# Attention visited once a turn, and three output tiles in front of the last operand, in a two-block fp32 transformer kernel on one core

## The chip, the cores and the metric

The kernel runs on one core of a Trainium2 chip, as one launch. Its time is the device time in microseconds (us); beside it stands the span of a profiled execution, from its first to its last instruction. Engines go by their short names: PE is the matrix engine (TensorE), DVE the vector engine, ACT the scalar engine, POOL GpSimd, SP the engine whose queue issues most DMAs.

## The reference

One sequence of 512 tokens with 1024 features goes through two blocks, all in float32. The first block has one layer:

```python
h = rms_norm(x, norm_mix); z = h @ w_in          # q, k, v of two attentions and two gates
y_a = windowed_gqa(q_a, k_a, v_a, sink)          # 8 heads, window of 128 on both sides
y_b = neighborhood_attn(q_b, k_b, v_b, rpb)      # 8 heads, 8 x 16 neighbourhood on an 8 x 64 grid
x = x + (gate_a * (y_a @ w_proj_a) + gate_b * (y_b @ w_proj_b)) @ w_out
x = x + square(relu(rms_norm(x) @ w_up)) @ w_down    # 4096 hidden features
```

and a norm at its end. The second block has two layers, each of which is

```python
x = x + 0.5 * swiglu(rms_norm(x), wg, wu, wd)    # 2816 hidden features
z = rms_norm(x) @ w_in                           # q, k, v, and three inputs of a convolution
attn = sliding_window_attention(q, k, v, sink)   # 8 query heads, 2 key heads, blocks of 128, causal
conv = b_gate * causal_conv3(c_gate * h_conv)
x = x + concatenate([attn, conv]) @ w_out
x = x + 0.5 * swiglu(rms_norm(x), wg, wu, wd)
```

and then a last norm.

## The kernel before

Activations lie with features on the 128 partitions and the 512 tokens along the free axis, in 8 blocks of features. To keep float32 accuracy every operand is split in two halves, a rounded high part and the rest as a low part (`wh`, `wl` for weights), and each product of blocks is three matmuls, high by high, high by low, low by high (L463 to L465 for a linear layer). A linear tile is 128 outputs by 512 tokens and sums over 8 operands, so it has 24 matmuls; it lies in one of three accumulator banks of PSUM (`acc`), or for the last tiles of an output linear in another.

Weights come in one stream in the order in which they are used. A tile has two items, each for four operands. An item is split by a cast on ACT (L389, the high half) and a subtraction on DVE (L391, the low half) into a pair of buffers of a ring of 7 (`RING`). The order of instructions on every engine is that in which the program issues them; nothing is reordered later. Splits are issued only in `split_to`: when a tile fetches an item, `item` asks for splits up to 5 items ahead (`AHEAD`), and `split_to` cuts this to 6 items behind the oldest item that is still in use. When the last item of a 512 KB unit is split, SP gets the DMA of a later unit, into one of 5 raw buffers.

`linear2` runs tiles side by side: all operands but the last `late` of each tile first, then the late operands of each tile, and then the evacuations. `out_linear` uses it for the first two tiles of an output linear (`ORDER` = 0, 1, 4, 2, 5, 3, 6, 7), with the last operand late; it runs the other six tiles one by one with `linear`, which issues a tile's matmuls, then what is due (the squares for the next norm), then its evacuation. There are three output linears: `wo` of the first block, with the operands in the order 0 to 7, and `0_wo` and `1_wo` of the second block's layers, with the operands in the order 4, 5, 6, 7 (convolution) and 0, 1, 2, 3 (attention). An evacuation (`ev_res`, L962) adds the tile to the residual `x` and then prepares the next feed-forward's operands (`prep_pairs`): for outputs 0 to 3 by four instructions on ACT (L656 to L661) and three on DVE, for outputs 4 to 7 by three on ACT (L666 to L672) and five longer ones on DVE (L667 to L674).

`run_attention` goes through the 16 steps of an attention in turns. A step is scores (`qk`, L782, which contract over 64 partitions, two heads at once), softmax (`soft` on ACT and its second half on DVE), transposes of the probabilities (`tr`, L823) and values (`pv_`, L843). In the second block (`late` true) a step's transposes come two turns behind its scores and its values three, so there are 19 turns. Between them PE works on the fill: the tiles of the other projections, cut in pieces of two operands (6 matmuls). Which pieces run where is set by shares of the total. A tile that ends goes on the list `evacs`, and `evacuate` issues its evacuation. A turn before the change is: scores; `evacuate`; fill up to half the turn's share; values; transposes; softmax; splits; the softmax's second half; fill up to the turn's share. The first block's two attentions run by the same function with `late` false.

Of the kernel before, what the change touches and what calls it, by code (L numbers as in the profile page):

```python
# [32 lines left out]
MID = 0.5  # L33
SLACK = (0.3, 0.2)
# [7 lines left out]
ORDER = [0, 1, 4, 2, 5, 3, 6, 7]  # L42
# [195 lines left out]
def two_blocks(ctx, tc, plan, xT, wstream, vecs, sinks, rpb_g, dists, masks, outT):  # L238
# [59 lines left out]
    def give(ids):  # L298
        for i in ids:
            if i in plain:  # L300
                plain.remove(i)
                use_slot(i, F32R)
        free.extend(ids)
        free.sort()
# [13 lines left out]
    for i in range(4):  # L318
        s = slot[7 * i:7 * i + 7]
# [50 lines left out]
    def split_item(idx):  # L370
        key, part = items[idx]
        combine(idx)
        h = wt_p.tile([P, S], F32R, tag="wh", name=f"wh{idx}")
        lo = wt_p.tile([P, S], F32R, tag="wl", name=f"wl{idx}")
        if blocks[key][0] is not None:
            (u, off), = where[key]
            k0, k1 = parts_of(key, part)
            src = raw[u][:, off + P * k0:off + P * k1]
        else:
            ra, rb = raw[where[key][0][0]], raw[where[key][1][0]]  # L380
            new = sums_of.get(key, {})
            if key[1] == "R":
                src = (ra, rb)[part % 2][:, S * (part // 2):S * (part // 2) + S]
            else:
                src = {1: ra[:, :S], 2: ra[:, S:], 4: rb[:, S:]}.get(part)
                if src is None:
                    src = new[{5: "s1", 6: "s2", 7: "s3", 3: "s4"}[part]]
        w = src.shape[1]
        nc.scalar.copy(h[:, :w], src)  # L389
        combine(idx + 1)  # L390
        nc.vector.tensor_tensor(lo[:, :w], src, h[:, :w].bitcast(F32), ALU.subtract)  # L391
        ready[idx] = (h, lo)
        for u, _ in where[key]:
            uses[u] -= 1
            if uses[u] == 0:
                raw.pop(u)
                freed.append(u)
        while freed and min(freed) == st["oldest"]:
            freed.remove(st["oldest"])
            st["oldest"] += 1  # L400
            load_unit()
# [4 lines left out]
    def split_to(idx):  # L406
        oldest = min(live) if live else st["next"]
        idx = min(idx, oldest + RING - 1, len(items) - 1)
        while st["split"] <= idx:
            split_item(st["split"])  # L410
            st["split"] += 1
# [81 lines left out]
    def flush():  # L493
        todo, deferred[:] = deferred[:], []
        for f in todo:
            f()

    def evacuate():
        todo, evacs[:] = evacs[:], []
        for _, f in todo:  # L500
            f()

    def linear(key, opnd, evac, pool=None, before=None):
        t = Tile(key, opnd, pool)
        t.mm(range(len(opnd)))
        run_due()
        flush()
        if before:
            before()
        evac(t.ps)  # L510
# [18 lines left out]
    def linear2(keys, opnd, evs, order, late, after=None, at=(0, 3)):  # L529


        n_e = len(order) - late
        t0 = Tile(keys[0], opnd)
        t0.mm(order[:n_e])
        t1 = Tile(keys[1], opnd)
        t1.mm(order[:n_e])
        if n_e:
            t0.mm(order[n_e:])
            t1.mm(order[n_e:])
        else:  # L540
            for part in range(2):
                t0.fetch(part)
                t1.fetch(part)
            for kc in order:
                t0.mm([kc])
                t1.mm([kc])
        if after:
            a, b = at
            t2 = Tile(keys[2], opnd)
            if a:  # L550
                t2.mm(order[:a])
            second = after()
            t2.mm(order[a:b])
            second()
            evs[0](t0.ps)
            evs[1](t1.ps)
            t2.mm(order[b:])
            evs[2](t2.ps)
        else:
            evs[0](t0.ps)  # L560
            evs[1](t1.ps)

    def ft(name):
        return ft_p.tile([P, S], F32, tag="ft", name=name)
# [189 lines left out]
    def preload(func):  # L754
        nc.scalar.activation(dummy, epst, func)
# [96 lines left out]
    def run_attention(steps, fillers, needs, head=1, late=False):  # L852

        n = len(steps)
        lag = LAG2 if late else LAG1
        slots = n + lag + 1
        hold = [] if late else [50, 51]
        assert all(i in free for i in hold)
        free[:] = [i for i in free if i not in hold]
        total = sum(f[1] for f in fillers)  # L860
        parts, have, cost = [], set(), [0.0]
        queue = list(fillers)

        def fill():
            if not parts:
                key, c, make = queue.pop(0)
                fs = make()
                parts.extend((key if i == len(fs) - 1 else None, c / len(fs), f) for i, f in enumerate(fs))
            key, c, f = parts.pop(0)
            cost[0] += c  # L870
            f()
            have.add(key)

        def fill_to(share, slack):
            while (queue or parts) and cost[0] < total * share - slack:
                fill()

        for _ in range(2 * head):
            fill()
        total -= cost[0]  # L880
        cost[0] = 0.0

        for s in range(slots):
            if s < n:
                while not set(needs(s)) <= have:
                    fill()
                if any(key[-len(k):] == k for k in needs(s) for key, _ in evacs):
                    evacuate()
                steps[s][0](steps[s][4])
            evacuate()  # L890
            fill_to((s + MID) / slots, SLACK[0])
            if s > lag:
                k = s - lag - 1
                steps[k][3](steps[k][4])
            if lag <= s < n + lag:
                steps[s - lag][2](steps[s - lag][4])
            if s < n:
                rest = steps[s][1](steps[s][4])
                split_to(st["next"] + 2)
                rest()  # L900
            fill_to((s + 1) / slots, SLACK[1])
        assert not queue and not parts
        evacuate()
        flush()
        give(hold)
# [54 lines left out]
    def ev_res(n, scale, prepare):  # L960
        def f(ps):
            nc.vector.scalar_tensor_tensor(x[n], ps, scale, x[n], ALU.mult, ALU.add)  # L962
            if prepare:
                prepare(n)
        return f
# [36 lines left out]
    late = []  # L1002
# [16 lines left out]
    qa, ya, yb, qb, kb, vb = {0: take(2)}, {}, {}, {}, {}, {}  # L1019
    ka, va = take(2), take(2)  # L1020
    linear2(MIX1_HEAD, xop, [ev_split(qa[0], QS), ev_split(ka), ev_v(va)], ar, KC, make_inv, (5, 7))
    ya_done = []

# [77 lines left out]
    def needs_ab(s):  # L1101
        c = s % 16 // 4
        if s < 16:
            return [("qa", c)] if c else []
        return [("qb", c), ("kb", c), ("vb", c)]

    run_attention([(*f_a, s) for s in range(16)] + [(*f_b, s) for s in range(16)],
                  [fill(k) for k in FILL_AB], needs_ab)

# [23 lines left out]
    LAST_POOL = {ORDER[-2]: (y_p, "y"), ORDER[-1]: (sp_p, "sp")}  # L1133

    def out_linear(prefix, op, order, scale, prepare, before):
        linear2([prefix + ("wo", n) for n in ORDER[:2]], op, [ev_res(n, scale, prepare) for n in ORDER[:2]], order, 1)
        for n in ORDER[2:]:
            linear(prefix + ("wo", n), op, ev_res(n, scale, prepare), LAST_POOL.get(n), before if n == ORDER[-1] else None)
        preload(AF.Sqrt)

# [252 lines left out]
    def mix2(l, before):  # L1393
        qs, ys, tmp = {0: take(2)}, {}, {}
        ks, vs = take(2), take(2)
        linear2([(l,) + k for k in MIX2_HEAD], xop, [ev_split(qs[0], QS), ev_split(ks), ev_v(vs)], ar, 1, make_inv)
        cs = [take(2, late=True) for _ in range(4)]
        nc.vector.tensor_tensor(inv2, inv, inv, ALU.mult)
# [23 lines left out]
        def fl(key):  # L1422
            def make():
                if key[0] == "q":
# [6 lines left out]
                             y_plain(ys, lambda c: qs[c] + (ks + vs if c == 3 else [])),  # L1431
                             alibi(f"c{l}", 384, 256), 1 + l, (-1, 0))
        run_attention([(*f_c, s) for s in range(16)], [fl(k) for k in FILL_C],
                      lambda s: [("q", s // 4)] if s >= 4 else [], late=True)
        both = [ys[c] for c in range(4)] + cs
        out_linear((l,), [pair_of(i) for i in both], [4, 5, 6, 7, 0, 1, 2, 3], 1.0,
                   lambda n: prep_pairs(n, vcols(("ffn2_norm_2", l))), before)
        for i in both:
# [75 lines left out]
```

## Time and profile before

| | |
|---|---|
| median of 3 runs | 2453.61 us (2453.45 to 2454.51) |
| profiled execution | 2451.71 us |
| its span | 2449.6 us, 39694 instructions |
| DMA | 239.47 MB, mean 98 GB/s |
| HBM read, written | 234.81 MB, 2.10 MB |

Weight loads (PEld) run beside matmuls (PE). A line of a timeline is one instruction, or several alike in a row merged (x4); its first number is the start, its second how long it took, and an engine's idle time ahead of it stands in square brackets at its end, with what it waited for. Matmuls are pipelined: the next one starts before the one ahead has ended, so it is the distances of starts that count. In windows PEclk is the granted clock as a share of 2.4 GHz.

### The profile page before, as it was taken

The numbers are of one execution on the slowest core, as the hardware profiler recorded it, in microseconds if no ns is written. First come the engines' busy times: TensorE is split into PE (matmuls) and PEld (weight loads), VectorE is DVE, ScalarE is ACT, GpSimd is POOL, SyncE is SP. The second block draws the span as 40 slices with busy tenths as digits, with TensorE's granted clock in tenths as the row PEclk, the third lists the DMA queues.
The fourth block names the chain that finished last, engine by engine and source line by source line (L and its number), as shares of the span: only waits on it lengthen the run. The fifth ranks groups of instructions, "written<-read, shape, count | busy, mean of one in ns | idle before, by whom it ended". The sixth has DMA issues, their size and how long they took to land.

```text
span 2449.6 us, 39694 instructions
## 1 busy us (share of the span) xinstructions
PE 2434.6 (99%) x15192; PEld 2173.5 (89%) x15192; DVE 1957.1 (80%) x3962; ACT 1258.7 (51%) x2736; POOL 11.6 (0%) x26
## 2 busy tenths in 40 slices
PE   9999999999999999999999999999999999999998
PEld 7888889999889999888899999899999888999997
DVE  7778578877689978768798888898787687988885
ACT  5454355544455545444565445665445444654454
POOL 0000000000000000000000000000000000000000
PEclk9999999999999999999999999999999999999999
DMA  4222432233332333322223333333323222233332
GB/s 162 72 91 90 121 109 82 95 102 97 105 103 87 108 101 102 111 92 70 87 83 100 101 102 111 101 99 96 114 88 115 95 69 78 81 103 106 107 94 80
DMA packets 74622, 239.47 MB, mean 98 GB/s; under 512 B 8768, under 2 KB 10816, under 8 KB 74432
## 3 DMA queue, kind: packets, MB, share of 16 engines
q1 hardware_dynamic: 71248, 228.49, 29.2%
q0 software_dynamic: 1600, 6.82, 0.9%
q8 instruction: 119, 1.95, 0.3%
q10 hardware_dynamic: 1584, 1.64, 0.2%
q14 instruction: 71, 0.58, 0.1%
HBM read 234.81 MB, written 2.10 MB: 97 GB/s over the span
## 4 chain that ended last, share of the span: by engine, by line
PE 95%; DVE 3%; ACT 1%; DMA 0%; issue 0%; DVEq 0%; SPq 0%; ACTq 0%
PE X L1166 7%; PE X L1168 7%; PE X L1167 7%; PE YZ L1166 5%; PE YZ L1168 5%; PE YZ L1167 5%; PE mlp_D L463 2%; PE mlp_D L464 2%; PE mlp_D L465 2%; PE 0, 'ffn1'_D L463 2%; PE 0, 'ffn2'_D L463 2%; PE 1, 'ffn1'_D L463 2%; PE 1, 'ffn1'_D L464 2%; PE 0, 'ffn2'_D L464 2%; PE 0, 'ffn1'_D L464 2%; PE 1, 'ffn1'_D L465 2%
## 5 line engine op out<-in xcount | busy, mean ns | idle before, releaser
L391 DVE TENSOR_TENSOR wl<-raw,wh 128x512 fp32r<-128x512 f32 (+2 forms) x890 | 533.7, 610 | 98.9 <-ACT wh L389 91.3
L389 ACT CAST wh<-raw 128x512 fp32r<-128x512 f32 (+2 forms) x890 | 470.9, 556 | 5.2 <-PE 0, 'ffn1'_D L464 1.0
L1166 PE MATMUL X<-r,wh 128*128 128x256 f32 x1568 | 443.2, 283 | 1.2 <-ACT g L1172 0.7
L1168 PE MATMUL X<-r,wl 128*128 128x256 f32 x1568 | 443.7, 283 | 0.0
L1167 PE MATMUL X<-r,wh 128*128 128x256 f32 x1568 | 443.6, 283 | 0.0
L389 ACT CAST wh<-s 128x512 fp32r<-128x512 f32 x392 | 242.7, 620 | 230.0 <-DVE s L368 225.4
L1166 PE MATMUL YZ<-r,wh 128*128 128x256 f32 x1176 | 333.5, 284 | 0.4
L1167 PE MATMUL YZ<-r,wh 128*128 128x256 f32 x1176 | 332.8, 283 | 0.0
L1168 PE MATMUL YZ<-r,wl 128*128 128x256 f32 x1176 | 332.7, 283 | 0.0
L391 DVE TENSOR_TENSOR wl<-s,wh 128x512 fp32r<-128x512 f32 x392 | 269.5, 687 | 67.2 <-ACT wh L389 65.5
L1166 PEld LDWEIGHTS X<-r,wh 128*128 128x128 f32 x1568 | 300.0, 191 | 11.2 <-ACT g L1172 1.1
L1167 PEld LDWEIGHTS X<-r,wh 128*128 128x128 f32 x1568 | 300.0, 191 | 9.1
L1168 PEld LDWEIGHTS X<-r,wl 128*128 128x128 f32 x1568 | 300.0, 191 | 0.0
L1166 PEld LDWEIGHTS YZ<-r,wh 128*128 128x128 f32 x1176 | 225.7, 192 | 1.1 <-ACT u L1178 1.0
L1167 PEld LDWEIGHTS YZ<-r,wh 128*128 128x128 f32 x1176 | 225.7, 192 | 0.0
L1168 PEld LDWEIGHTS YZ<-r,wl 128*128 128x128 f32 x1176 | 225.7, 192 | 0.0
L1180 ACT COPY g<-X 128x256 f32<-128x256 f32 x98 | 36.5, 373 | 137.5 <-PE X L1168 137.4
L1181 DVE TENSOR_TENSOR u<-u,g 128x256 f32<-128x256 f32 x98 | 41.6, 425 | 73.6 <-ACT g L1180 73.1
L463 PE MATMUL mlp_D<-r,wh 128*128 128x512 f32 x256 | 100.1, 391 | 0.0
L464 PE MATMUL mlp_D<-r,wh 128*128 128x512 f32 x256 | 100.1, 391 | 0.0
L465 PE MATMUL mlp_D<-r,wl 128*128 128x512 f32 x256 | 99.6, 389 | 0.0
L1176 ACT COPY u<-X 128x256 f32<-128x256 f32 x98 | 36.5, 373 | 96.6 <-PE X L1168 96.3
(436 smaller groups left out, 5246.7 us busy)
## 6 DMA issues: line engine op xcount, KB each, us to landing
raw<-in_w SPq DMA_DIRECT2D x318, 512.0 KB, 3.6
raw<-in_w SPq DMA_DIRECT2D x64, 384.0 KB, 3.4
raw<-in_w SPq DMA_DIRECT2D x32, 448.0 KB, 3.7
raw<-in_w SPq DMA_DIRECT2D x32, 320.0 KB, 2.9
raw<-in_w SPq DMA_DIRECT2D x32, 256.0 KB, 2.7
bb<-in_rpb POOLq DMA_DIRECT2D x12, 384.0 KB, 3.5
xt<-in_x POOLq DMA_DIRECT2D x8, 256.0 KB, 2.9
xt<-in_x SPq DMA_DIRECT2D x2, 512.0 KB, 6.5
```

Of the source, the lines that this page charges most:

```text
L389: nc.scalar.copy(h[:, :w], src)
L391: nc.vector.tensor_tensor(lo[:, :w], src, h[:, :w].bitcast(F32), ALU.subtract)
L463: nc.tensor.matmul(self.ps, h[:, c], hx, start=(self.n == 1), stop=False)
L464: nc.tensor.matmul(self.ps, h[:, c], lx, start=False, stop=False)
L465: nc.tensor.matmul(self.ps, lo[:, c], hx, start=False, stop=end)
L1166: nc.tensor.matmul(out, h[:, c], hx, start=first, stop=False, skip_group_check=skip)
L1167: nc.tensor.matmul(out, h[:, c], lx, start=False, stop=False, skip_group_check=skip)
L1168: nc.tensor.matmul(out, l[:, c], hx, start=False, stop=(k == 3), skip_group_check=skip)
L1176: nc.scalar.copy(u[:, lo], out)
L1180: nc.scalar.copy(g[:, hi], out)
L1181: nc.vector.tensor_tensor(u[:, hi], u[:, hi], g[:, hi], ALU.add)
```

## The change

Three places change. `linear2` takes a list of tiles instead of two (where it is given an `after`, it takes two as before). `out_linear` gives it three tiles instead of two. And in `run_attention`, for the second block alone, a turn becomes: values; transposes; scores; softmax; `evacuate`; splits; the softmax's second half; fill up to the turn's share. What a turn's scores need is still filled and evacuated ahead of all this.

```diff
         n_e = len(order) - late
-        t0 = Tile(keys[0], opnd)
-        t0.mm(order[:n_e])
-        t1 = Tile(keys[1], opnd)
-        t1.mm(order[:n_e])
+        ts = []
+        for key in keys[:2] if after else keys:
+            ts.append(Tile(key, opnd))
+            ts[-1].mm(order[:n_e])
         if n_e:
-            t0.mm(order[n_e:])
-            t1.mm(order[n_e:])
+            for t in ts:
+                t.mm(order[n_e:])
...
         else:
-            evs[0](t0.ps)
-            evs[1](t1.ps)
+            for ev, t in zip(evs, ts):
+                ev(t.ps)
...
-                steps[s][0](steps[s][4])
-            evacuate()
-            fill_to((s + MID) / slots, SLACK[0])
+                if not late:
+                    steps[s][0](steps[s][4])
+            if not late:
+                evacuate()
+                fill_to((s + MID) / slots, SLACK[0])
             if s > lag:
                 k = s - lag - 1
                 steps[k][3](steps[k][4])
             if lag <= s < n + lag:
                 steps[s - lag][2](steps[s - lag][4])
             if s < n:
+                if late:
+                    steps[s][0](steps[s][4])
                 rest = steps[s][1](steps[s][4])
+                if late:
+                    evacuate()
                 split_to(st["next"] + 2)
                 rest()
+            elif late:
+                evacuate()
             fill_to((s + 1) / slots, SLACK[1])
...
     def out_linear(prefix, op, order, scale, prepare, before):
-        linear2([prefix + ("wo", n) for n in ORDER[:2]], op, [ev_res(n, scale, prepare) for n in ORDER[:2]], order, 1)
-        for n in ORDER[2:]:
+        linear2([prefix + ("wo", n) for n in ORDER[:3]], op, [ev_res(n, scale, prepare) for n in ORDER[:3]], order, 1)
+        for n in ORDER[3:]:
             linear(prefix + ("wo", n), op, ev_res(n, scale, prepare), LAST_POOL.get(n), before if n == ORDER[-1] else None)
```

## Rows read from the trace of the kernel before

**Rows 1.** The page's engine shares: busy us, share of the span, instructions.

```profile
PE 2434.6 (99%) x15192; PEld 2173.5 (89%) x15192; DVE 1957.1 (80%) x3962; ACT 1258.7 (51%) x2736; POOL 11.6 (0%) x26
```

**Rows 2.** PE's waits: waiting, waited for, total us, times, longest.

```profile
PE spread L738 <- DVE vr L730: 2.0, 2, 1.2
...
PE 0_wo L464 <- DVE r L571: 0.2, 1, 0.2
```

**Rows 3.** Windows: length, then busy us of each engine, clock, DMA share, GB/s.

```profile
1069.00:1182.30 113.30, 113.30 (x609) 90.99 (x608) 90.36 (x268) 56.24 (x157) 0.00 (x0) 1.00 0.24 71
1182.30:1226.70 44.40, 44.05 (x193) 35.89 (x193) 32.59 (x57) 25.00 (x49) 0.00 (x0) 1.00 0.27 83
318.70:362.30 43.60, 43.60 (x194) 36.12 (x193) 34.35 (x59) 26.26 (x52) 0.91 (x2) 1.00 0.35 114
2440.00:2442.50 2.50, 0.83 (x6) 0.76 (x7) 2.05 (x8) 1.19 (x3) 0.00 (x0) 1.00 0.96 318
2442.70:2445.00 2.30, 0.79 (x4) 0.60 (x3) 1.47 (x5) 0.00 (x0) 0.00 (x0) 0.50 0.26 85
```

**Rows 4.** Timeline of PE in one turn of the second block's attention.

```profile
1112.08 0.39 PE L464 MATMUL 0_cc<-r,wh 128*128 128x512 f32 x1
1112.30 0.39 PE L465 MATMUL 0_cc<-r,wl 128*128 128x512 f32 x1
1112.62 0.62 PE L782 MATMUL sc<-r,r 64*128 64x256 f32 x6
...
1115.04 0.60 PE L823 MATMUL ptc<-ident,tc 128*128 128x128 f32 x4
1115.40 0.47 PE L463 MATMUL 0_ch<-r,wh 128*128 128x512 f32 x1
1115.71 0.40 PE L464 MATMUL 0_ch<-r,wh 128*128 128x512 f32 x1
1115.95 0.40 PE L465 MATMUL 0_ch<-r,wl 128*128 128x512 f32 x1
```

**Rows 5.** Timeline of PE: transposes in front of scores, first block.

```profile
90.98 0.60 PE L936 MATMUL vtr<-ident,evv 128*128 128x128 f32 x4
91.51 0.80 PE L782 MATMUL sa<-r,r 64*128 64x384 f32 x6
```

**Rows 6.** Timeline of DVE in the output linear of layer 0.

```profile
1185.25 1.29 DVE L391 TENSOR_TENSOR wl<-raw,wh 128x512 fp32r<-128x512 f32 x2
1193.70 0.69 DVE L962 SCALAR_TENSOR_TENSOR xt<-0_wo,xt 128x512 f32<-128x512 f32 x1 [7.16 <-PE 0_wo L465]
...
1195.83 0.68 DVE L962 SCALAR_TENSOR_TENSOR xt<-0_wo,xt 128x512 f32<-128x512 f32 x1
...
1202.09 0.68 DVE L962 SCALAR_TENSOR_TENSOR xt<-0_wo,xt 128x512 f32<-128x512 f32 x1
...
1205.71 1.29 DVE L391 TENSOR_TENSOR wl<-raw,wh 128x512 fp32r<-128x512 f32 x2
```

**Rows 7.** Timeline of ACT there.

```profile
1205.06 1.14 ACT L389 CAST wh<-raw 128x512 fp32r<-128x512 f32 x2
```

**Rows 8.** Timeline of PE there: first matmul of the fourth tile's second half.

```profile
1202.34 0.39 PE L463 MATMUL 0_wo<-r,wh 128*128 128x512 f32 x1
```

**Rows 9.** Tile `1_wo`: idle us of the engine before its instructions, times.

```profile
  PE 1_wo L465: 7.6, 2
```

**Rows 10.** Timeline of DVE in the first block's output linear.

```profile
329.28 0.69 DVE L962 SCALAR_TENSOR_TENSOR xt<-wo,xt 128x512 f32<-128x512 f32 x1 [3.94 <-PE wo L465]
```

**Rows 11.** Timeline of PE there: first matmul of the fifth tile.

```profile
340.64 0.39 PE L463 MATMUL wo<-r,wh 128*128 128x512 f32 x1
```

**Rows 12.** The page's DMA issues: times, KB each, us to landing.

```profile
raw<-in_w SPq DMA_DIRECT2D x318, 512.0 KB, 3.6
```

**Rows 13.** Timeline of PE at the kernel's end.

```profile
2439.07 0.28 PE L1272 MATMUL varp<-onec,inv 128*128 128x1 f32 x2
...
2442.51 0.98 PE L738 MATMUL spread<-identr,vr 128*128 128x128 f32 x4 [1.16 <-DVE vr L730]
```

More of the change, by code (lines that the diff above doesn't have):

```diff
@@ L532, in linear2 @@
         n_e = len(order) - late
-        t0 = Tile(keys[0], opnd)
-        t0.mm(order[:n_e])
-        t1 = Tile(keys[1], opnd)
-        t1.mm(order[:n_e])
+        ts = []
+        for key in keys[:2] if after else keys:
+            ts.append(Tile(key, opnd))
+            ts[-1].mm(order[:n_e])
         if n_e:
-            t0.mm(order[n_e:])
-            t1.mm(order[n_e:])
+            for t in ts:
+                t.mm(order[n_e:])
         else:
             for part in range(2):
-                t0.fetch(part)
-                t1.fetch(part)
+                for t in ts:
+                    t.fetch(part)
             for kc in order:
-                t0.mm([kc])
-                t1.mm([kc])
+                for t in ts:
+                    t.mm([kc])
         if after:
@@ L559, in linear2 @@
         else:
-            evs[0](t0.ps)
-            evs[1](t1.ps)
+            for ev, t in zip(evs, ts):
+                ev(t.ps)
     def ft(name):
```

## The prediction

> **What bounds the kernel now.** I read the engine shares first, then the list of waits of TensorE (PE), then the stretches, and last the order of single instructions. In the shares the reader is to see PE busy in 2434.6 of 2449.6 us [rows 1]: whatever the change does, it acts through gaps on PE, and some 15 us of gaps is all there is. The list of waits names almost none of them: the longest is 2.0 us at a spread, and in an output linear 0.2 us, for an operand split by VectorE (DVE) [rows 2]. In the stretches, the attention of the second block's first layer takes 113.3 us with PE busy all of it and DVE busy 90.4; the output linear behind it takes 44.4 with DVE busy 32.6; the first block's output linear takes 43.6 without a gap on PE [rows 3]. So nothing here waits for the last operand of an output linear, which is what the third tile in front of it is to cover: this part of the change has no wait to remove. All it can do is change what DVE and ScalarE (ACT) have in front of them when PE comes for the next weights.
>
> **Part 1, the attention once a turn.** No instruction is added or removed; PE's order in a turn goes from scores, fill, values, transposes, fill to values, transposes, scores, fill. A fill matmul starts 0.22 to 0.23 us after the one before. Before, the scores start 0.32 after a fill matmul; four transposes take 0.36 from their first start to the fill behind them; and that fill's second matmul comes 0.31 later instead of 0.23, its third 0.24 later [rows 4]. After, the scores come behind transposes. In the second block no such pair exists; the nearest rows are the four transposes of a value tile in front of the first block's scores, 0.53 us from first start to the scores [rows 5]. Old: 0.32 + 0.36 + 0.31 = 0.99. New: 0.53 + 0.23 (the fill matmul that now follows another) + 0.23 = 0.99. What is left is the slow restart behind the transposes, which goes: 0.01 at the third matmul, and a little at those behind it; I put it at 0.035 per turn. Turns 2 to 15 have both a transpose and scores, 14 in each of two layers: 28 x 0.035 = 1.0 us saved. Bounds: if transposes to scores cost no more than transposes to fill, another 0.53 - 0.36 = 0.17 goes each time, 28 x 0.205 = 5.7 us saved; if the scores pay both the way out of the transposes and the way in from a fill matmul, 0.36 + 0.32 = 0.68 instead of 0.53, 28 x (0.15 - 0.035) = 3.2 us lost. I take the 1.0, since rows 5 has the very pair of operations.
>
> The Trainium skill, page "TensorEngine Tiling (Array Packing)", section "Key Properties", says that going from one tiling of the array to another drains TensorE. The rows agree: scores use 64 of the 128 rows, and are entered and left with the extra spacing above. There are as many such switches after the change as before, one in and one out per turn, so by that rule nothing is saved and the sum below would be 1.0 us longer.
>
> Otherwise the order is covered: a probability tile is transposed two turns after its softmax, and its split is used a turn later, with 18 fill matmuls x 0.23 = 4.1 us of PE work between. DVE has 113.3 - 90.4 = 22.9 us free in the stretch [rows 3]. The evacuation of a fill tile moves behind the softmax, but three accumulator banks bear a turn's delay. I count nothing for these; if that cover failed, PE would wait at the value matmuls for what exceeds 4.1 us, perhaps 0.3 us a turn, 28 x 0.3 = 8 us.
>
> **Part 2, three tiles in front of the last operand.** Call the output tiles t0 to t7. PE's work is the same, and so is its order from t3 on. What moves is the ends: t0's evacuation can start only after seven more operands x 3 matmuls x 0.227 = 4.76 us, and t2's work stands with t0's and t1's in front of t3's weight splits in the queues of ACT and DVE. Before, t2's first item was fetched behind t1's evacuation, and this fetch issued the next splits.
>
> How many splits are there already? The ring has 7 pairs. In the second block the first operands are 4 to 7, so the open item of t0 is its first part, number i; splits reach i+6, which is t3's first half. The trace shows this stop: DVE makes two splits at 1185.25 and then sits idle for 7.16 us until t0 ends [rows 6]. So after the change t3's second half is split only behind the evacuations of t0, t1 and t2. In numbers, layer 0 [rows 6]: t0's evacuation at 1193.70 + 4.76 = 1198.46; t1's follows 1195.83 - 1193.70 = 2.13 later, t2's another 2.13 later, at 1202.72. t2 is output 4, one of the kind with the longer preparation: from 1202.09, where this evacuation starts now, to the first cast behind it at 1205.06 is 2.97 [rows 6, 7]. So the cast starts at 1205.69, and with its 0.6 PE has its high half at 1206.3. It needs it where it needs it now, as it has done as many matmuls by then: at 1202.34 [rows 8]. **PE waits 4.0 us.** Casts take 0.6 (two in a row 1.14) and the subtractions for the low half 0.65 (two in 1.29), and the first of these starts 0.65 behind the first cast's start [rows 6, 7]; so the low half is there 0.7 after the high half, while the third matmul wants it 0.45 after the first: 0.3 more. That is 4.3 us, and the same in layer 1, whose DVE sits idle as long before its tile ends (7.6 us in both gaps together) [rows 9]. 2 x 4.3 = 8.6.
>
> In the first block the operands come in their own order, the open item is t0's second part, i+1, and splits reach i+7: t3 is whole, t4 is what is missing. t0's evacuation: 329.28 + 4.76 = 334.04, t2's 4.26 later at 338.30, the cast 2.97 later at 341.27, done at 341.9. PE wants t4 at 340.64 [rows 10, 11]: 1.3 us, with 0.3 for the low half 1.6.
>
> What is late next: t3's bank is that of t0, free at 1198.46 + 0.69 = 1199.15, and PE gets to it half a tile, 12 x 0.227 = 2.72 us, before 1202.34, at 1199.62: no wait. After the stall DVE has six splits and three squares to catch up with, but it had 11.8 us free in this stretch [rows 3], and PE's stall gives it 4 more; I count nothing further. The weight loads are issued with the splits, so some go out up to 4 us later; one takes 3.6 us to land [rows 12] and five buffers lie ahead of the splits, of one tile (24 x 0.227 = 5.4 us) each. Hidden; with that cover gone up to 3.6 us a layer. Bounds of the part: 0, if the splits are there after all, to 8.6 + 1.6 + 2 x 3.6 = 17.4.
>
> **Sum.** 8.6 + 1.6 - 1.0 = 9.2 us on the profiled execution's 2451.71 (span 2449.6 and 2.1 around it): 2460.9. The median of the runs is 1.9 above that execution: 2462.8.
>
> **Rivals.**
> (a) The clock falls in the stalls. The trace holds the full clock through all its short gaps, but at its end, with only single-column matmuls from 2439.1 on, the granted clock goes from 1.00 to 0.50 (2.4 to 1.2 GHz) between 2442.5 and 2442.7 [rows 3, 13]. That is a nearly idle stretch of 3.5 us, and mine are 4.0 us without a matmul. Against it: one fall at one place, and block 1's stall is shorter. How long the clock takes to come back no row shows; if as long as it took to fall, 3.5 us at half pace lose 1.75 us per layer: 2462.8 + 3.5 = 2466.3. The Trainium skill, page "TensorE: Matmul & The Clock Gate", section "Why this matters for your kernels", warns of idle gaps between bursts of matmuls for this reason; the rows agree with the warning.
> (b) Not slower: the weights run ahead. If the splits behind t3's first half are issued before the three evacuations, or these leave ACT's and DVE's queues sooner, the stalls vanish and the attention's 1.0 remains: 2452.6. It decides from the point where the stalls sum to under 5.9 us (4.9 from the bound below and 1.0). For it: 7.16 us in which DVE has nothing to do, so there would be time. Against: the same 7.16 us, since with time at hand it made two splits and stopped.
> (c) The visits are worth their bound: 5.7 instead of 1.0 saved, stalls as worked out: 2458.1. Rows 5 speaks against. With (b) as well it would be 2447.9.
> (d) The attention gets waits of its own, 3.2 to 8 us, from DVE work that now lies in one clump: around 2468. Against: 22.9 us of free DVE.
>
> **How the numbers follow.** No change is within 0.2% of the median, 4.9 us either way (2448.7 to 2458.5), which is about what a measurement of this kernel can tell from none. My forecast 0.60, (a) 0.15, (b) 0.11, of it 0.04 with (c)'s saving too, (c) alone 0.07, (d) 0.07. Slower: 0.60 + 0.15 + 0.07 less 0.04 for stalls that come out at half their size, 0.78. Faster: 0.04, and 0.01 for what I don't see: 0.05. Same: the remaining 0.17. The range 2456.5 to 2468.5 holds the forecast, (a), (c) and most of (d); (b) is left out.
>
> **What would show it.** Right: a wait of PE of about 4 us in the middle of the fourth tile of each of the second block's output linears and of 1.3 us at the start of the first block's fifth, for the cast (L389) of a weight, with ACT and DVE busy with three evacuations in a row; the attention's stretches shorter by half a microsecond each; 0.53 us from four transposes to the scores. Wrong: no such waits, clocks below 1.00 behind them, PE waiting in the attention, or the attention shorter by more than 2 us a layer.

## The result, and the profile after

| | before | after |
|---|---|---|
| median | 2453.45 us (2453.16 to 2454.51, 5 runs) | 2475.94 us (2473.02 to 2476.12, 5 runs) |
| ratio, 95% interval | | 1.0088 (1.0077 to 1.0099) |
| profiled execution | 2451.71 us, span 2449.6 | 2476.12 us, span 2474.3 |

The change costs 22.5 us; the forecast was 9.2, so the direction was right and less than half of the size. The page's engine shares of the changed kernel, to be held against [rows 1]:

```profile
PE 2445.1 (99%) x15192; PEld 2182.5 (88%) x15192; DVE 1955.2 (79%) x3962; ACT 1259.2 (51%) x2736; POOL 11.6 (0%) x26
```

PE has the same 15192 matmuls and is busy 10.5 us longer with them, and the span less the busy time, the gaps, went from 15.0 to 29.2 us. Two things are to be looked for: where PE waits, and where its matmuls became slower. The waits, in the columns of [rows 2]:

```profile
PE 1_wo L463 <- ACT wh L389: 3.9, 1, 3.9
PE 0_wo L463 <- ACT wh L389: 3.9, 1, 3.9
PE 1_wo L463 <- ACT r L570: 2.1, 1, 2.1
PE 0_wo L463 <- ACT r L570: 2.1, 1, 2.1
...
PE wo L463 <- ACT wh L389: 1.1, 1, 1.1
PE yc L843 <- DVE r L960: 1.1, 2, 0.6
```

Three lines name a weight's cast (L389): the forecast waits, 3.9, 3.9 and 1.1 us. The other three new ones were not forecast: an output linear waits for the cast of an operand (L570), and the attention's values (`yc`) for the evacuation of a value tile (L960).

Windows of the changed kernel, in the columns of [rows 3]: the attention of layer 0, the output linear behind it and the first block's output linear, each the same stretch as there, and then four short ones.

```profile
1074.00:1188.50 114.50, 113.82 (x610) 92.51 (x608) 87.34 (x265) 55.73 (x156) 0.00 (x0) 1.00 0.24 70
1188.50:1242.20 53.70, 47.59 (x193) 37.90 (x192) 34.66 (x59) 25.59 (x51) 0.00 (x0) 0.94 0.23 71
318.86:364.20 45.34, 44.20 (x194) 35.97 (x193) 32.97 (x58) 25.25 (x51) 0.91 (x2) 1.00 0.36 110
...
728.90:735.70 6.80, 6.80 (x34) 6.80 (x34) 2.78 (x9) 1.77 (x5) 0.00 (x0) 0.50 0.32 92
1193.10:1196.50 3.40, 3.24 (x8) 2.42 (x8) 1.58 (x3) 0.69 (x2) 0.00 (x0) 0.50 0.39 94
1217.00:1220.40 3.40, 3.40 (x10) 2.62 (x9) 3.30 (x7) 2.94 (x6) 0.00 (x0) 0.50 0.73 217
2090.80:2094.20 3.40, 3.40 (x9) 2.63 (x9) 3.34 (x6) 3.14 (x6) 0.00 (x0) 0.50 0.65 229
```

The output linear of layer 0 grew by 9.3 us and its granted clock fell to 0.94. The short windows show where it fell: the clock is 0.50 (1.2 GHz) for 3.4 us behind the first wait (1193.1) and behind the second (1217.0), and in layer 1 behind the second only (2090.8). The fall at 728.9 lies between the blocks, where no line of the change runs; more of it below.

**The forecast wait.** PE, ACT and DVE at the fourth tile's second half, each a timeline:

```profile
1211.58 0.39 PE L465 MATMUL 0_wo<-r,wl 128*128 128x512 f32 x1
1215.82 0.50 PE L463 MATMUL 0_wo<-r,wh 128*128 128x512 f32 x1 [3.85 <-ACT wh L389]
...
1217.22 0.63 PE L464 MATMUL 0_wo<-r,wh 128*128 128x512 f32 x1
1217.64 0.63 PE L465 MATMUL 0_wo<-r,wl 128*128 128x512 f32 x1
```

```profile
1215.16 2.18 ACT L389 CAST wh<-raw 128x512 fp32r<-128x512 f32 x4
```

```profile
1207.93 0.69 DVE L970 SCALAR_TENSOR_TENSOR xt<-0_wo,xt 128x512 f32<-128x512 f32 x1 [13.25 <-PE 0_wo L465]
...
1210.06 0.68 DVE L970 SCALAR_TENSOR_TENSOR xt<-0_wo,xt 128x512 f32<-128x512 f32 x1
...
1212.19 0.68 DVE L970 SCALAR_TENSOR_TENSOR xt<-0_wo,xt 128x512 f32<-128x512 f32 x1
```

Three evacuations start 2.13 us apart, and ACT's cast comes 2.97 behind the third, 1215.16 - 1212.19, as worked out. DVE sat idle for 13.25 us ahead of them, where the splits could have been made ("splits first" below makes them there). From 1217.0 on, behind the wait, matmuls start 0.43 us apart instead of 0.227.

**The wait at an output linear's start.** PE and DVE there:

```profile
1188.50 0.39 PE L463 MATMUL 0_wo<-r,wh 128*128 128x512 f32 x1
...
1190.31 0.39 PE L465 MATMUL 0_wo<-r,wl 128*128 128x512 f32 x1
1192.80 0.57 PE L463 MATMUL 0_wo<-r,wh 128*128 128x512 f32 x1 [2.11 <-ACT r L570]
1193.53 0.80 PE L464 MATMUL 0_wo<-r,wh 128*128 128x512 f32 x1 [0.16 <-DVE r L571]
```

```profile
1186.72 0.43 DVE L960 TENSOR_TENSOR r<-yc,r 64x256 fp32r<-64x256 f32 x1 [0.44 <-ACT r L959]
1187.16 0.69 DVE L1419 TENSOR_TENSOR cc<-cc,0_ch 128x512 f32<-128x512 f32 x1
1188.64 0.75 DVE L1422 SCALAR_TENSOR_TENSOR cy<-cc,vec,cy 128x511 f32<-128x511 f32 x1 [0.79 <-ACT cy L1421]
1189.42 0.75 DVE L1423 SCALAR_TENSOR_TENSOR cy<-cc,vec,cy 128x510 f32<-128x510 f32 x1
...
1190.69 0.68 DVE L919 TENSOR_TENSOR cb<-0_cb,inv 128x512 f32<-128x512 f32 x1
...
1192.78 0.69 DVE L571 TENSOR_TENSOR r<-cb,r 128x512 fp32r<-128x512 f32 x1 [0.68 <-ACT r L570]
```

The linear's fourth operand is the last convolution block, made from three fill tiles (`0_cc`, `0_ch`, `0_cb`). The second of these (`0_ch`, L1419 to L1423) now has its evacuation behind the last turn's values and theirs (L960), so DVE is still in it when PE has ended the third (`0_cb`, last start 1188.27). The block's own evacuation (L919) starts at 1190.69, the operand's cast starts at 1192.13 and takes 0.62, and PE has had only three operands (2.0 us) to bridge it. In the kernel before, this last convolution of `cy` was done before the last value tile, and at 1182.54 DVE was ready for the third tile before PE:

```profile
1179.12 0.75 DVE L1415 SCALAR_TENSOR_TENSOR cy<-cc,vec,cy 128x510 f32<-128x510 f32 x1
1180.19 0.42 DVE L952 TENSOR_TENSOR r<-yc,r 64x256 fp32r<-64x256 f32 x1 [0.32 <-ACT r L951]
...
1182.54 0.69 DVE L911 TENSOR_TENSOR cb<-0_cb,inv 128x512 f32<-128x512 f32 x1 [0.16 <-PE 0_cb L465]
```

Even so the operand's two halves came just late there, and the matmuls around them lost 0.93 us in all; the 0.2 us for L571 in [rows 2] are a part of this. So the operand had no slack, and what delays it further is paid in full: about 2.0 us more per linear.

**The wait in the attention.** DVE and PE in a turn:

```profile
1135.31 0.68 DVE L1419 TENSOR_TENSOR cc<-cc,0_ch 128x512 f32<-128x512 f32 x1
1137.26 0.75 DVE L1422 SCALAR_TENSOR_TENSOR cy<-cc,vec,cy 128x511 f32<-128x511 f32 x1 [1.28 <-ACT cy L1421]
1138.05 0.75 DVE L1423 SCALAR_TENSOR_TENSOR cy<-cc,vec,cy 128x510 f32<-128x510 f32 x1
...
1139.64 0.68 DVE L391 TENSOR_TENSOR wl<-raw,wh 128x512 fp32r<-128x512 f32 x1
1140.24 0.41 DVE L960 TENSOR_TENSOR r<-yc,r 64x256 fp32r<-64x256 f32 x1
1141.08 0.43 DVE L960 TENSOR_TENSOR r<-yc,r 64x256 fp32r<-64x256 f32 x1 [0.43 <-ACT r L959]
```

```profile
1140.68 0.39 PE L465 MATMUL 0_cc<-r,wl 128*128 128x512 f32 x1
1141.66 0.75 PE L843 MATMUL yc<-r,r 128*128 128x256 f32 x3 [0.58 <-DVE r L960]
```

One turn hands DVE a convolution's evacuation and the softmax's second half (among the rows left out), and a value tile's evacuation stands behind both. DVE sits idle for 1.28 us in between, for an instruction on ACT (L1421) that stands behind the softmax there. Values have one bank, so the next ones come 0.98 us after the fill matmul instead of 0.22.

### The profile page after: what moved, and what is told of

Its sections match the earlier page's. It is cut to its first block, busy times and chain, and to the rows that moved or that the text cites. A ratio compares the mean times of both kernels' runs of the same rounds, so it can differ in the third digit from the quotient of the medians.

```text
span 2474.3 us, 39691 instructions
## 1 busy us (share of the span) xinstructions
PE 2445.1 (99%) x15192; PEld 2182.5 (88%) x15192; DVE 1955.2 (79%) x3962; ACT 1259.2 (51%) x2736; POOL 11.6 (0%) x26
## 3 DMA queue, kind: packets, MB, share of 16 engines
q1 hardware_dynamic: 71248, 228.49, 29.2%
## 4 chain that ended last, share of the span: by engine, by line
PE 87%; DVE 9%; ACT 3%; issue 1%; DMA 0%; DVEq 0%; SPq 0%; ACTq 0%
PE X L1174 7%; PE X L1176 7%; PE X L1175 7%; PE YZ L1174 5%; PE YZ L1176 5%; PE YZ L1175 5%; PE mlp_D L463 2%; PE mlp_D L464 2%; PE mlp_D L465 2%; DVE wl L391 2%; PE 1, 'ffn1'_D L463 2%; PE 0, 'ffn2'_D L463 2%; PE 0, 'ffn1'_D L463 2%; PE 0, 'ffn1'_D L464 2%; PE 0, 'ffn2'_D L464 2%; PE 1, 'ffn1'_D L464 2%
## 5 line engine op out<-in xcount | busy, mean ns | idle before, releaser
L389 ACT CAST wh<-raw 128x512 fp32r<-128x512 f32 (+2 forms) x890 | 470.2, 556 | 5.1 <-PE 0, 'ffn1'_D L464 1.0
L389 ACT CAST wh<-s 128x512 fp32r<-128x512 f32 x392 | 242.7, 620 | 230.3 <-DVE s L368 223.6
```

## The experiments

Every run stands beside runs of the kernel before on the same chip (medians 2453.33 to 2454.27). The table gives, by first and last matmul starts in the profiles, how many us longer than before each stage took ("between blocks" runs from the first block's last norm to the second block's first attention); "falls" is the number of stretches at half clock within it, 3.4 us each, or 6.8 where it says double. Line numbers in a run's rows are those of its own kernel, a few lines off those of the changed one.

| kernel | median us | ratio, 95% interval | `wo` | between blocks | attention, layer 0 / 1 | `0_wo` (falls) | `1_wo` (falls) |
|---|---|---|---|---|---|---|---|
| after | 2475.94 | 1.0088 (1.0077, 1.0099) | 1.73 | 3.06 | 1.19 / 1.05 | 9.35 (2) | 8.04 (1) |
| attention alone | 2461.32 | 1.0033 (1.0021, 1.0044) | 0.00 | 1.49 | 1.08 / 1.09 | 1.96 (0) | 3.57 (1) |
| three tiles alone | 2467.78 | 1.0061 (1.0046, 1.0076) | 1.69 | 1.51 | 0.00 / 0.00 | 6.67 (1, double) | 5.98 (1) |
| splits first | 2461.75 | 1.0036 (1.0022, 1.0049) | 0.00 | 0.00 | 1.18 / 1.05 | 3.60 (1) | 2.05 (0) |
| last turns' evacuations first | 2475.77 | 1.0093 (1.0078, 1.0108) | 1.72 | 0.00 | 4.90 / 4.79 | 6.81 (1, double) | 5.55 (1) |
| evacuations at once, two tiles | 2478.73 | 1.0101 (1.0086, 1.0116) | 0.00 | 3.07 | 12.41 / 12.29 | -0.05 (0) | 0.01 (0) |
| evacuations at once, splits first | 2477.34 | 1.0095 (1.0080, 1.0110) | 0.00 | 3.09 | 12.58 / 10.85 | 0.00 (0) | 0.20 (0) |
| three tiles alone, PE kept busy | 2463.60 | 1.0040 (1.0026, 1.0054) | 1.68 | 1.49 | 0.00 / 0.00 | 4.38 (0) | 4.43 (0) |
| before, one operand later | 2451.91 | 0.9993 (0.9985, 1.0002) | 0.00 | 3.05 | 0.00 / 0.00 | -0.96 (0) | -0.93 (0) |
| after, PE kept busy | 2471.12 | 1.0071 (1.0056, 1.0087) | 1.71 | 3.05 | 1.14 / 1.05 | 6.45 (0) | 6.39 (0) |
| splits first, one operand later | 2456.70 | 1.0010 (1.0001, 1.0019) | 0.00 | 1.49 | 1.13 / 1.07 | -0.02 (0) | -0.04 (0) |

**Attention alone.** The changed kernel with two tiles in `linear2`.

```diff
-        linear2([prefix + ("wo", n) for n in ORDER[:3]], op, ..., order, 1)
-        for n in ORDER[3:]:
+        linear2([prefix + ("wo", n) for n in ORDER[:2]], op, ..., order, 1)
+        for n in ORDER[2:]:
```

> The new turn order alone, with two tiles in front of the last operand. Theory A (the four costs of the change are separate: 4 us waits for a cast from the three tiles; 2.0 us at each start of a second-block output linear, because in the last turns a conv tile's evacuation stands behind the values; about 1.1 us in each attention; clock falls of 1.6 to 3.1 us behind the longer gaps): 2 x 1.1 + 2 x 2.0 = 6.2 us over before, 2459.7, and 1.6 more for each clock fall behind the two start gaps, to 2463. No wait for a cast (L389) in any output linear, no clock fall at the boundary of the two blocks. Rival B (the start gap belongs to the three tiles, which hold all accumulator banks): only the attention's 2.2 us, 2455.7, with start gaps of 0.9 us as before.

The start's wait is there without the three tiles:

```profile
PE 0_wo L463 <- ACT r L570: 2.1, 1, 2.1
PE 1_wo L463 <- ACT r L570: 2.1, 1, 2.1
```

So the operand is late by the turn's new order. In layer 0 no fall follows this wait, in layer 1 one does; the same gap can go either way.

**Three tiles alone.** The kernel before with the changed `linear2` and `out_linear`, and the old turn.

> The three tiles alone, with the old turn order. Theory A: 1.7 in the first block and 2 x 4.3 in the second, 10.3 us, 2463.8; 1.6 more for each of two clock falls behind the 4 us waits, and 3.1 if the stretch of single-column matmuls between the blocks, which starts as late as in the changed kernel, lets the clock fall again: up to 2470. Start gaps 0.9 us as before. Rival B: start gaps of 2.3 us here too, so 4 us more.

The attention and the starts are as before to 0.00 us, and the cast waits are whole (3.9, 3.9, 1.1). Behind the first the clock is down for twice as long:

```profile
1208.40:1215.20 6.80, 5.41 (x13) 4.22 (x14) 6.36 (x11) 5.11 (x10) 0.00 (x0) 0.50 0.52 159
```

**Splits first.** The changed kernel, with the splits of the next two items (in the second block the fourth tile's second half and the fifth's first) issued ahead of the three evacuations; `split_to` allows them there, since all matmuls of the three tiles are issued.

```diff
         else:
+            if len(ts) == 3:
+                split_to(st["next"] + 2)
             for ev, t in zip(evs, ts):
                 ev(t.ps)
```

> The changed kernel, but the splits of the next two items are issued ahead of the three evacuations. Theory A: the waits for a cast in the fourth and fifth tiles go, 1.7 + 2 x 4.2 = 10.1 us and the clock falls behind them; left are the attention and the start gaps: 2459.7 to 2463, as in the kernel with the attention alone. The boundary between the blocks is reached as early as before the change, and no clock fall there. Rival C (the fourth tile waits because the three evacuations themselves are too much for DVE, whatever the order): the waits move to the next tile's weights and the time stays over 2470.

The three cast waits are gone from the list and the first block's output linear is back to 0.00. ACT makes one of the casts in the time in which it sat idle:

```profile
1195.66 0.62 ACT L389 CAST wh<-raw 128x512 fp32r<-128x512 f32 x1 [5.79 <-PE 0_wo L464]
```

The cause of these waits is thereby shown: the order of issue on ACT and DVE, not a lack of their time.

**Last turns' evacuations first.** In the turns without scores the evacuations go ahead of the values.

```diff
+            if late and s >= n:
+                evacuate()
             if s > lag:
```

> The changed kernel, but in the last three turns, which have no scores, the evacuation of the fill is issued ahead of the values. Theory A: the start gaps of both second-block output linears go back from 2.5 to 0.9 us, 2 x 2.0 = 4 us, and with the clock fall behind the first of them 5.6: 2470 to 2472 instead of 2475.9; the waits for a cast stay at 1.1, 3.9 and 3.9. Rival B: no change, 2476.

A miss. The wait at the linear's start is gone, but the last turns' values wait in its place, with one clock fall in each attention, and the attention costs 4.9 instead of 1.2 us in layer 0, the fall included:

```profile
PE yc L843 <- ACT r L570: 3.3, 2, 1.6
```

**Evacuations at once.** Each fill tile's evacuation is issued with its last piece, none behind the softmax; two tiles in `linear2`.

```diff
             f()
             have.add(key)
+            if late:
+                evacuate()
...
                 rest = steps[s][1](steps[s][4])
-                if late:
-                    evacuate()
                 split_to(st["next"] + 2)
                 rest()
-            elif late:
-                evacuate()
```

> The new turn order with two tiles in front of the last operand, but a fill tile's evacuation is issued right behind the piece that ends it, instead of behind the next turn's softmax. Theory A (the evacuation's late place makes both the start gaps and the attention's waits): start gaps back from 2.5 to 0.9 us, no wait of the values for DVE, and the 0.5 us per layer that one pass of PE a turn saves comes out: 2452.4 against 2453.4 before, 9 us under the kernel with the attention alone (2461.3). Rival D (the new order packs ACT's and DVE's attention work into one clump, and some wait remains wherever the evacuation stands): 2455 to 2459, with waits at the values or at the start.

A second miss, in the attention: the output linears are as before, and the values wait far more, with two clock falls in each attention.

```profile
PE yc L843 <- DVE r L958: 8.1, 6, 2.3
PE yc L843 <- ACT r L570: 4.7, 4, 1.6
```

This shows the evacuation's place as the cause at the linear's start, and refutes the expectation that it is the whole cause in the attention. Before the longest of these waits a value tile's evacuation (L958, from 1117.29) again comes behind a fill tile's (L917, from 1114.59). How much of the attention's waits is the fill's evacuation, and how much the clump of scores, softmax and values in one visit, was not separated.

**Evacuations at once, splits first.** The same with three tiles and the fourth tile's splits ahead of the evacuations.

> The changed kernel with both mends: evacuations right behind the piece that ends a tile, and two splits ahead of the three evacuations. Theory A: three tiles in front of the last operand then cost nothing and bring nothing, since no wait for the last operand was there: 2452.4, the same as with two tiles. Rival E (the third tile has a worth of its own that the waits hid): 1 us or more under the kernel with two tiles.

The three tiles cost 0.0 to 0.2 us then, and bring nothing. Of the three places tried for the fill tiles' evacuations (behind the softmax, ahead of the last turns' values, at once) the change's own is the cheapest by the attention and the linear's start together, and none is free.

**Three tiles alone, PE kept busy.** 16 matmuls of ones into a spare bank lie in the middle of the fourth tile in the second block, where PE waits; they are no part of the result.

```diff
+            t.mm(range(4))
+            idle = bank("idle")
+            for _ in range(FILLER):
+                nc.tensor.matmul(idle[:, :P], ones, ones, start=True, stop=True)
+            t.mm(range(4, 8))
```

> The three tiles alone with the old turn order, and 16 matmuls of ones into a spare bank (3.4 us, no part of the result) in the middle of the fourth tile of the second block's output linears, where PE waits 3.9 us for a cast. Theory A (a part of the loss is the clock, which falls behind the waits because PE does nothing in them): the wait is filled, no clock fall behind it; 1.6 us per 3.4 us of half clock come back, so 2463.5 to 2464.5 instead of 2467.8, while the first matmul of the second half comes as late as before. Rival F (the clock falls for another reason, or its falls cost nothing): 2467.8 or more.

The linears grow by 4.4 us each, about the wait alone, and the clock holds in the wait and behind it:

```profile
1208.00:1214.00 6.00, 5.72 (x30) 4.49 (x29) 5.85 (x11) 5.17 (x11) 0.00 (x0) 1.00 0.41 123
1214.00:1230.00 16.00, 16.00 (x72) 13.23 (x72) 13.30 (x24) 10.07 (x21) 0.00 (x0) 1.00 0.42 121
```

By medians 4.2 us came back (3.8 by the table), with work added: what a wait costs beyond its own length is the clock. The Trainium skill, page "TensorE: Matmul & The Clock Gate", section "Why this matters for your kernels", warns of gaps between bursts of matmuls for this reason, and these two kernels agree.

**Before, one operand later.** The kernel before, with the last convolution operand seventh instead of fourth in the second block's output linears.

```diff
-        out_linear((l,), ..., [4, 5, 6, 7, 0, 1, 2, 3], 1.0,
+        out_linear((l,), ..., [4, 5, 6, 0, 1, 2, 7, 3], 1.0,
```

> The kernel before, with one list changed: the second block's output linears take the last conv operand seventh instead of fourth (4, 5, 6, 0, 1, 2, 7, 3). Theory A: the one gap that an output linear did have before the change, at its fourth operand (0.9 us a layer, counted with the restart), is covered by three more operands of PE work (2.0 us): 2 x 0.9 = 1.9 us under before, 2451.5, without touching the turn order or the number of tiles. Rival G (the gap comes from the weights behind it in DVE's queue, not from the operand): no change, 2453.4.

Each linear loses the 0.93 us at its late operand. The total's interval just reaches 1 (11 and 15 runs), so a version that beats both kernels is likely but not established.

**After, PE kept busy.** The changed kernel with 10 such matmuls behind the third operand and 16 in the fourth tile.

> The changed kernel with matmuls of ones into a spare bank (no part of the result) where PE waits in the second block's output linears: 10 (2.1 us) at the start gap, 16 (3.4 us) in the middle of the fourth tile. Theory A (of the 22.5 us, 16.4 are waits: 1.7 + 2 x 4.3 in the output linears' tiles, 2 x 2.0 at their starts, 2 x 1.1 in the attention; the other 6 are falls of the clock behind them): the waits are filled but not shortened, and the falls go: 2453.4 + 16.4 = 2469.8. Rival F (the 6 us are something else): 2475.9.

The clock holds through both linears, and the two take 4.6 us less than in the changed kernel (4.8 by medians).

**Splits first, one operand later.** Both edits in the changed kernel.

> The changed kernel with the fourth tile's splits ahead of the three evacuations, and the last convolution operand moved from the fourth to the seventh place of the second block's output linears. Theory A: the 2.0 us gaps of the splits-first kernel are only the late evacuation of that one operand, which comes 4.2 us after the linear's first matmul; three more operands in front of it are 3 x 3 x 0.227 = 2.0 us, so the gap goes but for 0.1 to 0.3 us, no clock fall follows, and the output linears come 0.7 to 0.9 us shorter than before, as with this order alone (-0.95). With the attention's +1.1 per layer left that is 2 x (1.1 - 0.8) = +0.6 us: about 2454 to 2455, within 0.2% of the kernel before. Rival B: the gap belongs to the queue as a whole, and the next operand or weight is late in its turn: 1 to 2 us per output linear stay, 2457 to 2459.

Between the two. The long gap at the start is gone and no fall follows, but the operand is still just late, at its new place:

```profile
1189.85 0.39 PE L465 MATMUL 0_wo<-r,wl 128*128 128x512 f32 x1
1190.34 0.50 PE L463 MATMUL 0_wo<-r,wh 128*128 128x512 f32 x1
1191.07 0.50 PE L464 MATMUL 0_wo<-r,wh 128*128 128x512 f32 x1 [0.23 <-DVE r L573]
```

The high half is 0.27 us late, as expected; its low half 0.5 more, which the expectation forgot. That is about the 0.93 us of the kernel before, so the linears come out even with it and the attention's 2.2 us stay; 2456.7 against 2453.57 is 3.1, and the other 0.9 lies in no stage of the change.

## Why the prediction was wrong in size

The profiled executions allow a sum: `wo` 1.73, attention 2.24, `0_wo` 9.35, `1_wo` 8.04, together 21.4 us. (The 3.06 between the blocks is left out: the stretch comes and goes with the same code there, see below.) By cause, the cast waits and the clock from the two kernels with PE kept busy, the others from the stages and waits above:

| | forecast | shown |
|---|---|---|
| cast waits in the second block, low half included | 8.6 | 2 x 4.4 = 8.8 |
| cast wait in the first block | 1.6 | 1.7 |
| the attention's order | -1.0 | -1.0 |
| waits at and behind the attention's values | 0 | 1.7 + 1.5 = 3.2 |
| waits at the output linears' start | 0 | 2 x 2.0 = 4.0 |
| clock falls behind these waits | 0 in the forecast, 3.5 as rival (a) | 2.9 + 1.65 = 4.6 (three stretches) |

- **The three tiles: right.** The reading of the ring, the evacuations' pace and the cast's place held to 0.2 us in all three output linears, and rival (b) is out: with 13.25 us at hand DVE made no split. "Splits first" shows the mechanism by taking it away. Nothing further came from the weight loads or the banks.
- **The attention's order: right.** Transposes to scores take the 0.53 us of [rows 5]:

```profile
1106.21 0.60 PE L823 MATMUL ptc<-ident,tc 128*128 128x128 f32 x4
1106.74 0.63 PE L782 MATMUL sc<-r,r 64*128 64x256 f32 x6
```

  In layer 0 the starts at and within values and transposes are 1.7 us further apart in all while the stretch is 1.2 longer, so 0.5 came back (and as much in layer 1); the reading by which the switches leave nothing saved is out, and so is rival (c).
- **The step that failed: "The evacuation of a fill tile moves behind the softmax, but three accumulator banks bear a turn's delay. I count nothing for these".** The banks did bear it; no fill tile waits for one. What gave way are two things behind the evacuation. In the attention PE waits at the values for DVE, 1.7 and 1.5 us in the two layers: 1.0 of layer 0's is the turn shown above, with the value tile's evacuation behind a convolution's and a single bank for values; the rest is smaller delays in other turns, of which the largest (0.3 us) waits for a split of the probabilities (L571). That the evacuation's new place alone makes these waits is argued from the rows and not shown, since "evacuations at once" did not remove them. And the evacuation of the last-but-one fill tile moves past the last values, where its user is the output linear's fourth operand: 2.0 us a layer, which "attention alone", "last turns' evacuations first" and "evacuations at once" show. The 22.9 free us of DVE [rows 3] were no answer, since they are a total over 113 us and the lateness is that of one turn's queue. This is the mechanism of rival (d), which put all of its 3.2 to 8 us into the attention; the runs show 3.2 there and 4.0 outside, 7.2 together, and that the sum lies in its range is in part luck. "Attention alone" shows both parts without the tiles.
- **The clock: the mechanism and price of rival (a), with too low a chance.** It costs 1.5 us per stretch of 3.4 us, against 1.75 for an assumed 3.5; a stretch of 6.8 us, which also occurs, was not thought of. But it follows the 2.5 us gap at a linear's start too, at times, and at 0.15 it stood as the exception. "PE kept busy" shows its share twice. (a) and (d) were also treated as alternatives, though longer gaps make falls likelier: the two together on top of the forecast are 9.2 + 7.2 + 4.6 = 21.0, near the 21.4.
- **The base.** I took the 1.9 us from the profiled execution of before to the median as a constant. That execution is one of the fastest group of runs and has no clock fall between the blocks; what makes the other groups slower is not shown (last section).
- **A misreading.** The 2.0 us at the spread [rows 2] are the total of two waits, the longer of them 1.2, and not the longest wait. Nothing in the sum rests on it.

What stays open: what share the evacuation's place has in the attention's waits, why the gap at a linear's start brings a fall in one layer and none in the other, and why a stretch lasts 3.4 or 6.8 us.

## What to carry to other kernels

When an evacuation moves, list what is issued behind it on its engine and each user's slack, the last turn's too: a share of free time over a long stretch says nothing of one turn's queue. When tiles are held open together, issue the next tile's weight splits ahead of their evacuations. And a wait of PE is to be priced with a stretch of half clock behind it, 1.5 us here for one of 3.4 us and 2.3 for the one of 6.8 in "three tiles alone": the waits of 3.9 us that were left empty were all followed by one, those of 1.6 to 2.3 us in some places only.

## What had not been expected of the hardware

The clock also falls where PE has no gap. Between the blocks PE runs matmuls of one or two columns for a norm's sum. The stretch in the profile of before, then the microsecond of the changed kernel in which its fall begins (the rest of the fall is the window from 728.90 above):

```profile
721.00:734.00 13.00, 13.00 (x103) 12.49 (x102) 9.23 (x24) 5.74 (x13) 0.00 (x0) 1.00 0.23 77
```

```profile
728.00:729.00 1.00, 1.00 (x11) 1.00 (x10) 0.00 (x0) 0.00 (x0) 0.00 (x0) 0.94 0.00 0
```

PE is busy throughout by the records of both kernels, and in one of them at half clock for 6.8 us. Over the kernels' profiles this stretch is 0, 3.4 or 6.8 us long and costs 0, 1.5 or 3.05 us, also in "attention alone" and "before, one operand later", where every instruction ahead of it is that of the kernel before. The runs of the kernel before lie in three groups, 2451.4 to 2451.9, 2453.0 to 2453.8 and 2454.1 to 2454.9 us. Their mean clocks are 0.999 in the first, mostly 0.997 in the second and mostly 0.998 in the third. The first fits an execution without this stretch, as the profiled one; but the slowest group does not have the lowest clock, so the three lengths do not explain the groups by themselves. The kernel's start varies too: in four of the profiles the clock is at half for 3.4 us somewhere between 7.3 and 12.1 us, and over all of them the first matmul of `wo` lies up to 1.7 us later than in the profile of before. What decides this was not tried.
